# Differential keys and queries rounded on all 128 rows and placed by transfers inside SBUF

## The chip, the cores and the metric

The kernel runs on one core of one Trainium2 chip. The metric is the device time of one execution in microseconds, lower is better. Three executions of the kernel before took 2180.04, 2183.42 and 2184.76 us; their median is 2183.42 us.

## The reference

A hybrid diffusion backbone of two layers over 256 latent tokens with 256 context tokens ahead of them, width 1024. Each layer is a half-step SwiGLU feed-forward, a token mixer of two parallel branches (retention with 4 heads, differential attention with 8 heads) and another half-step feed-forward. The change lies in the keys and queries of the differential attention:

```python
def diff_attend(q, k, v, lam):
    s = jnp.einsum('bhiqd,bhikd->bhiqk', q, k).astype(jnp.float32) * (DIFF_DH ** -0.5)
    p = jax.nn.softmax(s, axis=-1)
    a = p[:, :, 0] - lam * p[:, :, 1]
    return jnp.einsum('bhqk,bhke->bhqe', a.astype(v.dtype), v)

q_d = rope_2d(to_diff_heads(dq), row, col)
k_d = rope_2d(to_diff_heads(dk), row, col)
k_dc = to_diff_heads(dkc)
k_all = jnp.concatenate([k_dc, k_d], axis=3)
```

A head has two conditions of 64 channels (the two softmax maps). Latent queries and keys are rotated in pairs of channels (a 2-D rotary embedding), context keys are not. Latent tokens read context and latent keys, context tokens context keys alone. The second layer needs no context output, so there only latent tokens have queries.

## The kernel before

**Arithmetic.** TensorE multiplies in a rounded 32-bit type. A float32 operand x is split into a rounded part H and the rest Lo = x - H, and a product is three matmuls into one PSUM bank (`mm3`, L340 to L342: H times H, H times Lo, Lo times H). Weights are loaded in 512 KB tiles by SP's queue (`load`, L147) and split by a ScalarE cast (L154) and a VectorE subtraction (L155); four raw tiles and five split tiles are in flight.

**The mixer.** `projT` (L646 ff.) makes channels x tokens blocks with the weight as the stationary operand; 48 matmuls fill one pair of PSUM banks (`main4`), which `ev` then empties, and the pair goes back to the next user. `tok` and `wide` make tokens x channels blocks with the activations as the stationary operand, 24 matmuls for a bank. The differential attention works in four blocks u = 0..3 of two heads. `diff_blocks(u)` projects and evicts K for all 512 tokens and then Q; `diff_attn` (L766 ff.) then makes for each 128 queries of a head a *score* (L781, L782: both conditions, hi and lo of the keys; L783 row maximum on VectorE; L786 two exponentials on ScalarE; L790, L792, L794 the combination of the two maps on VectorE), a *turn* (L803 transposes, L805 copy on ScalarE) and a *weigh* (L815 matmuls with V; after the last one of a block L823 square, L825 sum, L827, L829 power on GpSimd, L834 scaling). Scores, turns and weighs use the other PSUM pairs (`side4`).

**The eviction that the change touches.** In `ev_diff` (L685 to L700) the 128 rows of a block are condition 0 of a head in rows 0 to 63 and condition 1 in rows 64 to 127. For a score, the query tile of condition m holds the rounded query in 64 rows and its rest in the other 64, and the key tile holds the rounded key in both halves (and its rest in both halves of a second tile), so that two matmuls give the whole product. So each condition of K is written by a copy (L696), a subtraction (L697) and two copies into the other half (L698, L699), and each condition of Q by an activation (L692) and a subtraction into the other half (L693). Latent rows pass through `rotate` (L668, L671, L673) first, which multiplies rows with their swapped partners in pieces of 32 rows (four L671 for one block).

**What sets the order.** Work is written with deferred pieces (`defer`, `tick`, `flush`), and then a scheduler places each engine's instructions in one fixed sequence when the program is built. An engine runs its sequence in order; a matmul that waits holds all that stand behind it on TensorE. In a mixer of layer 0 the sequence of the Python code is: K(0), Q(0), deferred attention 0, `rv_block(0)` (a wide block of 96 matmuls), `rkq_blocks(0)` (the retention's key and query projections), and so on for u = 1; then K(2), Q(2), attention 2, a wide block; K(3), Q(3), attention 3, two wide blocks.

The lines that decide when the pair of a K block comes free:

```python
            for c in pairs:
                ev(c, bk[:, :, c * 256:(c + 1) * 256])
            main4.put(b0)
            tick(w)
```

Of the kernel before, what the change touches and what calls it, by code (L numbers as in the profile page):

```python
# [11 lines left out]
F32 = mybir.dt.float32  # L12
F32R = mybir.dt.float32r
BF16 = mybir.dt.bfloat16
AF = mybir.ActivationFunctionType
ALU = mybir.AluOpType
# [18 lines left out]
def build(ctx, tc, a):  # L35
# [536 lines left out]
    def mixer(l, st, AB, fetch, nxt):  # L572
# [69 lines left out]
        def projT(b, pairs, ev, w):  # L642
            ws = [split(r) for r in load(a["winT"][l, b])]
            n = 256 * len(pairs)
            if len(pairs) == 2:
                b0 = main4.two()  # L646
                bk = b0
            else:
                b0 = main4.one()
                bk = b0.rearrange("p (j n) -> p j n", j=2)  # L650
            for j in range(2):
                js = slice(j * P, (j + 1) * P)
                for k in range(KD):
                    wt = ws[k // 4].rearrange("p s (k n) -> p s k n", k=4)
                    mm3(bk[:, j], wt[:, 0, k % 4, js], wt[:, 1, k % 4, js], h[k // 2][:, k % 2, 0, 0:n],
                        h[k // 2][:, k % 2, 1, 0:n], k == 0, k == KD - 1)
                    if k == 7 and j == 0:
                        flush()
                    if j * KD + k in ((3, 7, 11) if len(pairs) == 2 else (7,)):
                        tick(w)  # L660
            for c in pairs:
                ev(c, bk[:, :, c * 256:(c + 1) * 256])
            main4.put(b0)
            tick(w)

        def rotate(b, tab, half):
            q, w = tmp2([P, 2, 256]), tmp2([P, 2, 256])
            dve.tensor_tensor(out=q, in0=b, in1=tab[:, 0].unsqueeze(1).broadcast_to([P, 2, 256]), op=ALU.mult)  # L668
            for p0 in range(0, P, half):
                p1 = p0 ^ half  # L670
                dve.tensor_tensor(out=w[p0:p0 + half], in0=b[p1:p1 + half],  # L671
                                  in1=tab[p0:p0 + half, 1].unsqueeze(1).broadcast_to([half, 2, 256]), op=ALU.mult)
            dve.tensor_tensor(out=q, in0=q, in1=w, op=ALU.add)  # L673
            return q
# [7 lines left out]
                                         op0=ALU.mult, op1=ALU.subtract)  # L682
            return ev

        def ev_diff(H, Lo):  # L685
            def ev(c, b):
                q = rotate(b, dtab, 32) if c == LAT else b
                sl = slice(c * 256, (c + 1) * 256)
                for m in range(2):
                    own, oth = slice(64 * m, 64 * m + 64), slice(64 - 64 * m, 128 - 64 * m)  # L690
                    if Lo is None:
                        act(H[m][own, :, sl], q[own], AF.Copy, scale=0.125)  # L692
                        dve.scalar_tensor_tensor(out=H[m][oth, :, sl], in0=q[own], scalar=0.125,  # L693
                                                 in1=H[m][own, :, sl], op0=ALU.mult, op1=ALU.subtract)
                    else:
                        nc.scalar.copy(H[m][own, :, sl], q[own])  # L696
                        dve.tensor_tensor(out=Lo[m][own, :, sl], in0=q[own], in1=H[m][own, :, sl], op=ALU.subtract)  # L697
                        nc.scalar.copy(H[m][oth, :, sl], q[own])  # L698
                        nc.scalar.copy(Lo[m][oth, :, sl], Lo[m][own, :, sl])  # L699
            return ev  # L700

        def ev_V(dst):
# [289 lines left out]
        def diff_blocks(u, before=None):  # L992
            KH = [slot([P, 2, 512], F32R) for _ in range(2)]
            KL = [slot([P, 2, 512], F32R) for _ in range(2)]
            projT(8 + u, BOTH, ev_diff(KH, KL), 0.3)
            if before:
                before()
            Q = [slot([P, 2, 512], F32R) for _ in range(2)]
            projT(4 + u, QP, ev_diff(Q, None), 0.3)
            return KH, KL, Q  # L1000

        def diff_defer(u, kq, dv, within):
# [223 lines left out]
def rope_tables():  # L1226
    def ang(pos, half):
        inv = (np.float32(10000.0) ** (-np.arange(half, dtype=np.float32) / np.float32(half))).astype(np.float32)
        return (pos.astype(np.float32)[:, None] * inv[None, :]).astype(np.float32)

    t = np.arange(T)
    r = ang(t, 64)
    c, s = np.cos(r), np.sin(r)
    rt = np.stack([np.concatenate([c, c], 1), np.concatenate([-s, s], 1)], 0)
    d = np.concatenate([ang(t // 64, 16), ang(t % 64, 16)], 1)
    c, s = np.cos(d), np.sin(d)
    dt = np.stack([np.concatenate([c, c, c, c], 1), np.concatenate([-s, s, -s, s], 1)], 0)

    def lay(z):
        return np.ascontiguousarray(z.transpose(2, 0, 1), dtype=np.float32)  # L1240
    return lay(rt), lay(dt)
# [6 lines left out]
def layout(i):  # L1248
    f = {k: np.asarray(v) for k, v in i.items()}
    a = {}  # L1250
    a["xin"] = np.concatenate([f["x"][0], f["ctx"][0]], 0).reshape(4, P, D)
    a["ccc"] = np.stack([f["c"][0], f["c_ctx"]], 1).reshape(KD, P, 2).transpose(1, 0, 2)
    a["sel"] = (np.arange(P)[:, None] % 32 == np.arange(2)[None, :]).astype(np.float32)
    a["wada0"] = f["w_ada"][0, :, 0:2 * D].reshape(KD, P, 2, 4, 256).transpose(3, 1, 0, 2, 4).reshape(4, P, 4096)
    a["cc"] = np.stack([f["c"][0], f["c_ctx"]], 0)
    a["wada"] = f["w_ada"].transpose(0, 2, 1).reshape(L, 36, 2, P, D).transpose(0, 1, 3, 2, 4).reshape(L, 36, P, 2 * D)
    a["bada"] = f["b_ada"].reshape(L, 9, 8, P).transpose(3, 0, 1, 2)
    a["nwc"] = f["norm_w"].reshape(L, 6, 8, P).transpose(3, 0, 1, 2)
    a["fin"] = (f["ffn_w_in"].reshape(L, 2, KD, P, 2, NF, P).transpose(0, 1, 5, 3, 2, 4, 6)
                .reshape(L, 2, NF, P, 2048))  # L1260
    a["fout"] = f["ffn_w_out"].reshape(L, 2, NF // 2, 2, P, D).transpose(0, 1, 2, 4, 3, 5).reshape(L, 2, NF // 2, P, 2048)
    cols = np.arange(8192)
    cols[3072:5120] = cols[3072:5120].reshape(32, 2, 2, 16).transpose(0, 2, 1, 3).reshape(-1)
    wi = f["w_in"][:, :, cols].reshape(L, KD, P, 32, 256)
    a["winT"] = wi[:, :, :, TB].transpose(0, 3, 2, 1, 4).reshape(L, 12, P, 2048)
    a["winW"] = wi[:, :, :, WB].reshape(L, KD, P, 10, 512).transpose(0, 3, 2, 1, 4).reshape(L, 10, P, 4096)
    a["wout"] = f["w_out"].reshape(L, 4, 2, P, D).transpose(0, 1, 3, 2, 4).reshape(L, 4, P, 2048)
    a["gnw"] = f["ret_gn_w"]
    a["subw"] = f["diff_subln_w"]
    a["lamv"] = f["diff_lambda"]  # L1270
    a["decay"] = f["ret_decay_logit"].reshape(L, 8)
    a["rtab"], a["dtab"] = rope_tables()
    a["strip"] = strip_table()
    return {k: np.ascontiguousarray(v) for k, v in a.items()}
# [16 lines left out]
```

## Time and profile before

| | before |
|---|---|
| median of 3 runs | 2183.42 us (2180.04 to 2184.76) |
| the profiled execution, own time | 2185.12 us |
| its span | 2183.3 us |
| granted TensorE clock, mean | 0.994 |
| TensorE busy (matmul) | 2140.8 us, 98% |
| VectorE busy | 1364.9 us, 63% |
| ScalarE busy | 859.4 us, 39% |
| GpSimd busy | 108.8 us, 5% |
| DMA | 306.98 MB, 141 GB/s, 41.1% of 16 engines on SP's queue |

Busy time is the sum of an engine's instructions; a matmul row shows a longer time (0.39 us for 512 columns) than the distance to the next one, since matmuls are pipelined. A timeline row has the start, the duration, engine, line, operation, tiles, and in brackets the idle time ahead of it on its engine with what ended it. In a windows row each engine's busy time stands with its number of instructions, then the granted TensorE clock (1.00 is 2.4 GHz, 0.50 is 1.2 GHz), the busy share of the DMA engines and GB/s.

### The profile page before, as it was taken

What the parts mean: (1) busy time and instruction counts of PE and PEld (TensorE: products, weight loads), DVE (VectorE), ACT (ScalarE), POOL (GpSimd) and SP (SyncE); (2) the same over time, 40 slices, a digit from 0 to 9 for tenths busy, and PEclk for the clock granted to TensorE, in tenths of its full rate; (3) what the DMA queues carried; (4) which work ended last, traced back from release to release, by engine and by line L of the source; (5) the groups of instructions that cost most, each with busy time, mean ns of one, the idle gap of its engine ahead of it and who ended that gap; (6) DMA issues with size and microseconds to landing.
All of it is one profiled execution on the core that took longest, in us unless ns stands there. A gap on an engine that the chain in (4) does not pass through costs nothing. (4 is left out here: it accounts for less than half of the span.)

```text
span 2183.3 us, 27485 instructions
## 1 busy us (share of the span) xinstructions
PE 2140.8 (98%) x10736; PEld 1792.6 (82%) x10736; DVE 1364.9 (63%) x2119; ACT 859.4 (39%) x1331; POOL 108.8 (5%) x194
## 2 busy tenths in 40 slices
PE   7999999999999999999999999999999999999998
PEld 5888888878788878888888888888888888878997
DVE  3799372677665874596233279825347776787554
ACT  3322232553534553432233252223235554565453
POOL 1000000101010000100000010000010000000000
PEclk9999999999999999999999999999999999999999
DMA  8866243222123234465234246733323323356554
GB/s 331 280 214 227 98 145 98 81 68 78 61 87 100 71 103 137 140 201 170 97 112 149 97 161 225 270 97 131 101 67 110 116 86 111 106 164 232 184 185 133
DMA packets 85058, 306.98 MB, mean 141 GB/s; under 512 B 9968, under 2 KB 10048, under 8 KB 84928
## 3 DMA queue, kind: packets, MB, share of 16 engines
q1 hardware_dynamic: 81936, 296.78, 41.1%
q0 software_dynamic: 2848, 8.43, 1.5%
q8 instruction: 84, 1.38, 0.3%
q14 instruction: 46, 0.38, 0.0%
q10 hardware_dynamic: 144, 0.01, 0.0%
HBM read 304.10 MB, written 1.09 MB: 140 GB/s over the span
## 5 line engine op out<-in xcount | busy, mean ns | idle before, releaser
L155 DVE TENSOR_TENSOR w<-raw,w 128x1024 fp32r<-128x1024 f32 x399 | 486.2, 1222 | 456.0 <-ACT w L154 452.9
L154 ACT CAST w<-raw 128x1024 fp32r<-128x1024 f32 x399 | 419.1, 1055 | 660.7 <-PE ps L342 598.2
L340 PE MATMUL ps<-h,w 128*128 128x512 f32 (+1 forms) x1820 | 652.7, 359 | 5.1 <-ACT w L154 3.0
L341 PE MATMUL ps<-h,w 128*128 128x512 f32 (+1 forms) x1820 | 652.2, 359 | 0.4 <-DVE h L293 0.3
L342 PE MATMUL ps<-h,w 128*128 128x512 f32 (+1 forms) x1820 | 651.4, 358 | 0.6 <-DVE w L155 0.6
L340 PEld LDWEIGHTS ps<-h,w 128*128 128x128 f32 x1820 | 345.2, 190 | 58.4 <-DVE h L292 4.6
L342 PEld LDWEIGHTS ps<-h,w 128*128 128x128 f32 x1820 | 345.7, 190 | 50.1 <-DVE w L155 1.3
L341 PEld LDWEIGHTS ps<-h,w 128*128 128x128 f32 x1820 | 345.7, 190 | 49.9 <-DVE h L293 1.4
L174 DVE CUSTOM_DVE_ANT_0 jd<-r,r 128x1024 bf16<-128x1024 f32 x224 | 273.4, 1220 | 5.8 <-DMA r<-wada_dram 1.6
L340 PE MATMUL ps<-w,h 128*128 128x512 f32 (+1 forms) x552 | 219.0, 398 | 16.3 <-ACT r L698 11.7
L341 PE MATMUL ps<-w,h 128*128 128x512 f32 (+1 forms) x552 | 216.8, 393 | 1.0 <-DVE w L155 1.0
L342 PE MATMUL ps<-w,h 128*128 128x512 f32 (+1 forms) x552 | 216.8, 393 | 0.0
L340 PE MATMUL ps<-w,gs 128*128 128x512 f32 x504 | 196.2, 389 | 0.0
L341 PE MATMUL ps<-w,gs 128*128 128x512 f32 x504 | 196.1, 389 | 0.0
L342 PE MATMUL ps<-w,gs 128*128 128x512 f32 x504 | 196.1, 389 | 0.0
L403 ACT ACTIVATE t<-ps 128x512 f32<-128x512 f32 (+1 forms) x85 | 46.7, 550 | 248.4 <-PE ps L342 248.4
L340 PEld LDWEIGHTS ps<-w,h 128*128 128x128 f32 x552 | 104.4, 189 | 39.8 <-ACT r L698 15.1
L341 PEld LDWEIGHTS ps<-w,h 128*128 128x128 f32 x552 | 104.4, 189 | 21.1 <-DVE w L155 2.3
L342 PEld LDWEIGHTS ps<-w,h 128*128 128x128 f32 x552 | 104.3, 189 | 20.9 <-DVE h L293 0.4
L404 DVE TENSOR_TENSOR r<-ps,t 128x512 f32<-128x512 f32 (+1 forms) x85 | 53.5, 629 | 104.1 <-PE ps L342 76.8
L340 PEld LDWEIGHTS ps<-w,gs 128*128 128x128 f32 x504 | 94.6, 188 | 20.0
L341 PEld LDWEIGHTS ps<-w,gs 128*128 128x128 f32 x504 | 94.6, 188 | 19.6
(199 smaller groups left out, 2184.4 us busy)
## 6 DMA issues: line engine op xcount, KB each, us to landing
raw<-fin_dram SPq DMA_DIRECT2D x176, 512.0 KB, 4.4
r<-wada_dram SPq DMA_DIRECT2D x144, 512.0 KB, 5.4
raw<-fout_dram SPq DMA_DIRECT2D x88, 512.0 KB, 3.6
raw<-winW_dram SPq DMA_DIRECT2D x80, 512.0 KB, 3.6
raw<-winT_dram SPq DMA_DIRECT2D x48, 512.0 KB, 3.6
raw<-wout_dram SPq DMA_DIRECT2D x16, 512.0 KB, 5.2
r<-scr POOLq DMA_DIRECT2D x10, 512.0 KB, 5.5
r<-cc_dram SPq DMA_DIRECT2D x7, 512.0 KB, 5.4
```

Of the source, the lines that this page charges most:

```text
L154: keep(nc.scalar.copy(w[:, 0, :], src))
L155: keep(dve.tensor_tensor(out=w[:, 1, :], in0=src, in1=w[:, 0, :], op=ALU.subtract))
L174: dve.tensor_tensor_reduce(out=junk, in0=r[j], in1=cs[c], scale=1.0, scalar=0.0, op0=ALU.mult, op1=ALU.add, accum_out=out[:, c, 2 * u + j: ...
L340: mm(o, lhsT=wH, rhs=xH, start=start, stop=False)
L341: mm(o, lhsT=wH, rhs=xL, start=False, stop=False)
L342: mm(o, lhsT=wL, rhs=xH, start=False, stop=stop)
L403: act(sg[:, :N], ab[0][:, :N], AF.Silu)
L404: dve.tensor_tensor(out=g[f // 2][:, f % 2, :N], in0=ab[1][:, :N], in1=sg[:, :N], op=ALU.mult)
```

## The change

The channels of the differential Q and K weight columns are permuted on the host, so that a block's rows are four groups of 32: condition 0, condition 1, condition 0, condition 1 (`rows_of`), and the partner of a row in the rotation is 64 rows away. `rotate` then needs two L671 instead of four. `ev_full` rounds all 128 rows at once: one activation and one subtraction for each of context and latent. The 32-row groups are then put where the scores want them by transfers from SBUF to SBUF on SP's queue (`move`): six moves of two transfers for K (128 KB each), four moves of two for Q; the third K move overwrites rows that the first two read. Q's rounded rows and rests go through two more slots of the big ring (qH, qL). `projT` evicts the context columns first, the latent ones after. No matmul is added or removed.

```diff
-            for c in pairs:
+            for c in reversed(pairs):
                 ev(c, bk[:, :, c * 256:(c + 1) * 256])
...
-        def ev_diff(H, Lo):
+        def rows_of(m):
+            return [slice(32 * m + 64 * x, 32 * m + 64 * x + 32) for x in range(2)]
+
+        def move(dst, md, src, ms, n):
+            for rd, rs in zip(rows_of(md), rows_of(ms)):
+                nc.sync.dma_start(dst[rd, :, 0:n].bitcast(F32), src[rs, :, 0:n].bitcast(F32))
+
+        def ev_full(H, Lo, scale):
             def ev(c, b):
-                q = rotate(b, dtab, 32) if c == LAT else b
+                q = rotate(b, dtab, 64) if c == LAT else b
                 sl = slice(c * 256, (c + 1) * 256)
-                for m in range(2):
...
+                act(H[:, :, sl], q, AF.Copy, scale=scale)
+                dve.scalar_tensor_tensor(out=Lo[:, :, sl], in0=q, scalar=scale, in1=H[:, :, sl],
+                                         op0=ALU.mult, op1=ALU.subtract)
             return ev
...
-            projT(8 + u, BOTH, ev_diff(KH, KL), 0.3)
+            projT(8 + u, BOTH, ev_full(KH[0], KL[0], 1.0), 0.3)
+            for K2 in (KH, KL):
+                move(K2[1], 1, K2[0], 1, 512)
+                move(K2[1], 0, K2[0], 1, 512)
+                move(K2[0], 1, K2[0], 0, 512)
...
-            projT(4 + u, QP, ev_diff(Q, None), 0.3)
+            qH, qL = slot([P, 2, 512], F32R), slot([P, 2, 512], F32R)
+            projT(4 + u, QP, ev_full(qH, qL, 0.125), 0.3)
+            for m in range(2):
+                move(Q[m], m, qH, m, 256 * NQ)
+                move(Q[m], 1 - m, qL, m, 256 * NQ)
+            slots.put(qH, qL)
             return KH, KL, Q
```

In the changed kernel the attention's lines are one lower than before (L782 is the maximum, L793 the combination, L802 the transposes, L804 the copy, L814 the weigh, L824 the sum), the moves are L690, the evictions' activation and subtraction L696 and L697.

TensorE, layer 0, u = 0: the first scores. Before, they stand 35 matmuls behind the Q projection (names: `ps` is PSUM, `w` a split weight, `h` the activations, the numbered `r` are slots of the big ring):

```order
L340 MATMUL ps<-w,h 128x512
L341 MATMUL ps<-w,h 128x512
L781 MATMUL ps<-r_3118,r_3204 128x512 [waits DVE_49]
L782 MATMUL ps<-r_3120,r_3204 128x512
L781 MATMUL ps<-r_3119,r_3205 128x512 [waits DVE_49]
L782 MATMUL ps<-r_3121,r_3205 128x512
```

Now they wait on the transfers, and stand behind 96 matmuls of the wide block and 4 of the next projection:

```order
L342 MATMUL ps<-w,h 128x512
L340 MATMUL ps<-h,w 128x512 [waits DVE_49]
L341 MATMUL ps<-h,w 128x512
L342 MATMUL ps<-h,w 128x512
L340 MATMUL ps<-h,w 128x512
L780 MATMUL ps<-r_3118,r_3202 128x512 [waits DMAHW4_49,DMAHW7_49,DMAHW1_49,DMAHW0_49]
L781 MATMUL ps<-r_3120,r_3202 128x512 [waits DMAHW6_49,DMAHW5_49]
```

So the block's eight scores moved from the wide block into the retention's key and query projections behind it.

TensorE, the same block's end: the last weigh. Before, it has projection matmuls on both sides, 17 ahead of it and 60 behind it:

```order
L340 MATMUL ps<-h,w 128x512
L341 MATMUL ps<-h,w 128x512
L342 MATMUL ps<-h,w 128x512
L815 MATMUL ps<-r_2895,t_3597 128x128 [waits Activation_49]
L815 MATMUL ps<-r_2895,t_3597 128x128
L340 MATMUL ps<-h,w 128x512
L341 MATMUL ps<-h,w 128x512
```

Now the last two turns and weighs follow each other, and the wide block of the retention's gates comes directly behind, waiting for VectorE:

```order
L342 MATMUL ps<-h,w 128x512
L802 MATMUL ps<-ident,t_3535 128x128 [waits DVE_49,Activation_49]
L802 MATMUL ps<-ident,t_3535 128x128
L814 MATMUL ps<-r_2895,t_3593 128x128 [waits Activation_49]
L814 MATMUL ps<-r_2895,t_3593 128x128
L802 MATMUL ps<-ident,t_3567 128x128 [waits DVE_49]
L802 MATMUL ps<-ident,t_3567 128x128
L814 MATMUL ps<-r_2895,t_3599 128x128 [waits Activation_49]
L814 MATMUL ps<-r_2895,t_3599 128x128
L340 MATMUL ps<-w,h 128x512 [waits DVE_49]
```

VectorE at that place now. The L340 above waits for the second L671 here, the last reading of the pair of the retention's key block; ahead of it stands the sum L824, which waits for ScalarE's square of the last weigh:

```order
L793 SCALAR_TENSOR_TENSOR t_3567<-t_3567,r_3572 128x256 [waits DVE_49]
L681 SCALAR_TENSOR_TENSOR r_3689<-ps,r_3688 128x2x256 [waits Activation_49]
L155 TENSOR_TENSOR w<-raw,w 128x1024 [waits DMAHW3_49,Activation_49]
L668 TENSOR_TENSOR t_3680<-ps,rtab 128x512
L824 TENSOR_REDUCE oss<-t_3653 128x4 [waits Activation_49]
L671 TENSOR_TENSOR t_3681<-ps,rtab 64x512
L826 SCALAR_TENSOR_TENSOR ms<-oss,es 128x4 [waits DVE_49]
L671 TENSOR_TENSOR t_3681<-ps,rtab 64x512
L833 SCALAR_TENSOR_TENSOR r_3661<-ps,rr,sub 128x128 [waits PE_49,Pool_49]
```

Before, the sum and the scaling of the block are done on VectorE ahead of that eviction:

```order
L155 TENSOR_TENSOR w<-raw,w 128x1024 [waits DMAHW4_49,Activation_49]
L825 TENSOR_REDUCE oss<-t_3651 128x4 [waits Activation_49]
L827 SCALAR_TENSOR_TENSOR ms<-oss,es 128x4 [waits DVE_49]
L834 SCALAR_TENSOR_TENSOR r_3659<-ps,rr,sub 128x128 [waits PE_49,Pool_49]
L834 SCALAR_TENSOR_TENSOR r_3659<-ps,rr,sub 128x128 x3
L668 TENSOR_TENSOR t_3676<-ps,rtab 128x512 [waits PE_49]
L671 TENSOR_TENSOR t_3677<-ps,rtab 64x512 x2
```

So the sum of the block moved from ahead of the eviction of the retention's keys into the middle of it. TensorE, layer 1, u = 2, the end of the attention now (K(3) and Q(3) are projected ahead of it, a wide block follows):

```order
L342 MATMUL ps<-h,w 128x256
L802 MATMUL ps<-ident,t_14177 128x128 [waits DVE_49]
L802 MATMUL ps<-ident,t_14177 128x128 x3
L814 MATMUL ps<-r_13741,t_14229 128x128 [waits Activation_49]
L814 MATMUL ps<-r_13741,t_14229 128x128
L814 MATMUL ps<-r_13742,t_14229 128x128 x2
L802 MATMUL ps<-ident,t_14201 128x128 [waits DVE_49]
L802 MATMUL ps<-ident,t_14201 128x128 x3
L814 MATMUL ps<-r_13741,t_14239 128x128 [waits Activation_49]
L814 MATMUL ps<-r_13741,t_14239 128x128
L814 MATMUL ps<-r_13742,t_14239 128x128 x2
L340 MATMUL ps<-w,h 128x512 [waits DVE_49]
```

Before, the last weigh there stands 59 matmuls ahead of that wide block:

```order
L815 MATMUL ps<-r_13725,t_14219 128x128 [waits Activation_49]
L815 MATMUL ps<-r_13725,t_14219 128x128
L815 MATMUL ps<-r_13726,t_14219 128x128 x2
L340 MATMUL ps<-h,w 128x512
L341 MATMUL ps<-h,w 128x512
```

So this attention's last turns and weighs moved behind both projections.

## Rows read from the trace of the kernel before

**Rows 1.** The page, part 1: busy time, share of the span, instructions.

```profile
PE 2140.8 (98%) x10736; PEld 1792.6 (82%) x10736; DVE 1364.9 (63%) x2119; ACT 859.4 (39%) x1331; POOL 108.8 (5%) x194
```

**Rows 2.** Waits of TensorE: line, releaser, us in total, times, longest.

```profile
PE ps L340 <- ACT r L698: 11.7, 8, 1.7
PE ps L340 <- DVE t L671: 3.2, 1, 3.2
```

**Rows 3.** Timeline of TensorE in layer 0, u = 0: the Q projection's end.

```profile
446.48 0.39 PE L340 MATMUL ps<-h,w 128*128 128x512 f32 x1
...
446.93 0.39 PE L342 MATMUL ps<-h,w 128*128 128x512 f32 x1
...
448.97 0.50 PE L340 MATMUL ps<-w,h 128*128 128x512 f32 x1 [1.65 <-ACT r L698]
```

**Rows 4.** Timeline of TensorE in layer 1: two long waits and what follows.

```profile
1916.15 0.60 PE L340 MATMUL ps<-w,h 128*128 128x512 f32 x1 [3.16 <-DVE t L671]
1917.58 0.80 PE L340 MATMUL ps<-w,h 128*128 128x512 f32 x1 [0.82 <-ACT r L698]
1918.17 0.63 PE L341 MATMUL ps<-w,h 128*128 128x512 f32 x1
...
1922.44 0.63 PE L342 MATMUL ps<-w,h 128*128 128x512 f32 x1
...
1966.17 0.66 PE L982 MATMUL ps<-ident,t 128*128 128x128 f32 x4 [2.05 <-DVE t L975]
```

**Rows 5.** Windows around a short and the two long waits.

```profile
445.00:455.00 10.00, 8.35 (x37) 6.58 (x36) 7.11 (x9) 6.37 (x11) 0.00 (x0) 1.00 0.18 55
...
1918.00:1921.00 3.00, 3.00 (x8) 2.33 (x8) 2.85 (x4) 1.88 (x4) 0.00 (x0) 0.50 0.36 98
...
1965.00:1970.00 5.00, 3.83 (x14) 3.14 (x15) 4.92 (x6) 3.63 (x6) 0.00 (x0) 0.75 0.97 326
```

**Rows 6.** Windows over four attentions: layer 0 u = 0, 2, 3, layer 1 u = 3.

```profile
457.00:497.00 40.00, 39.87 (x212) 31.90 (x212) 26.08 (x52) 20.99 (x51) 1.95 (x1) 1.00 0.17 55
...
717.00:752.00 35.00, 34.83 (x191) 27.92 (x191) 27.90 (x59) 19.74 (x49) 1.04 (x1) 1.00 0.13 41
778.00:815.00 37.00, 36.32 (x200) 28.99 (x200) 29.56 (x58) 21.18 (x52) 3.06 (x3) 1.00 0.28 87
...
1922.00:1943.00 21.00, 20.85 (x110) 16.80 (x109) 16.68 (x26) 13.49 (x28) 0.00 (x0) 0.97 0.43 137
```

**Rows 7.** Groups of instructions: count, busy us, mean ns, idle before.

```profile
L155 DVE TENSOR_TENSOR w<-raw,w 128x1024 fp32r<-128x1024 f32 x399 | 486.2, 1222 | 456.0 <-ACT w L154 452.9
...
L671 DVE TENSOR_TENSOR t<-ps,dtab 32x512 f32<-32x512 f32 x64 | 44.0, 687 | 0.9
...
L699 ACT CAST r<-r 64x512 fp32r<-64x512 f32 x32 | 19.8, 618 | 0.5
...
L697 DVE TENSOR_TENSOR r<-ps,r 64x512 fp32r<-64x512 f32 x16 | 11.0, 689 | 13.4 <-ACT r L696 13.1
L671 DVE TENSOR_TENSOR t<-ps,rtab 64x512 f32<-64x512 f32 x16 | 11.0, 688 | 0.2
...
L825 DVE TENSOR_REDUCE oss<-t 128x4 f32<-128x512 f32 x12 | 8.1, 679 | 2.1 <-ACT t L823 2.1
...
L823 ACT ACTIVATE t<-ps 128x512 f32<-128x512 f32 x12 | 7.2, 596 | 1.6 <-PE ps L815 1.6
...
L964 DVE SCALAR_TENSOR_TENSOR t<-t,ps 128x512 f32<-128x512 f32 x6 | 4.1, 682 | 0.6 <-ACT t L963 0.5
```

**Rows 8.** DMA issues: KB each, median us to landing; one issue's time.

```profile
raw<-winT_dram SPq DMA_DIRECT2D x48, 512.0 KB, 3.6
...
out_dram<-X SPq DMA_DIRECT2D x4, 256.0 KB, 2.1
rtab<-rtab_dram SPq DMA_DIRECT2D x1, 256.0 KB, 11.2
...
1979.84 0.33 SPq L163 DMA_DIRECT2D r<-cc_dram  x1
```

More of the change, by code (lines that the diff above doesn't have):

```diff
@@ L683, in ev_ret @@
             return ev
-        def ev_diff(H, Lo):
+        def rows_of(m):
[4 more added lines that the diff above has]
+        def ev_full(H, Lo, scale):
             def ev(c, b):
-                q = rotate(b, dtab, 32) if c == LAT else b
+                q = rotate(b, dtab, 64) if c == LAT else b
                 sl = slice(c * 256, (c + 1) * 256)
-                for m in range(2):
[L690 to L699, printed above, removed]
+                act(H[:, :, sl], q, AF.Copy, scale=scale)
+                dve.scalar_tensor_tensor(out=Lo[:, :, sl], in0=q, scalar=scale, in1=H[:, :, sl],
+                                         op0=ALU.mult, op1=ALU.subtract)
             return ev
@@ L1236, in rope_tables @@
     c, s = np.cos(d), np.sin(d)
-    dt = np.stack([np.concatenate([c, c, c, c], 1), np.concatenate([-s, s, -s, s], 1)], 0)
+    dt = np.stack([np.concatenate([c, c, c, c], 1), np.concatenate([-s, -s, s, s], 1)], 0)
     def lay(z):
@@ L1262, in layout @@
     cols = np.arange(8192)
-    cols[3072:5120] = cols[3072:5120].reshape(32, 2, 2, 16).transpose(0, 2, 1, 3).reshape(-1)
+    cols[3072:5120] = cols[3072:5120].reshape(16, 2, 2, 2, 16).transpose(0, 3, 1, 2, 4).reshape(-1)
     wi = f["w_in"][:, :, cols].reshape(L, KD, P, 32, 256)
```

## The prediction, made before the changed kernel ran

> **What bounds the kernel now.** I read the busy times first. TensorE works 98% of the span, VectorE 63%, ScalarE 39% [rows 1]: only what makes TensorE wait, or slows its clock, moves the time; work saved on the two others is worth nothing by itself. So the second view is what TensorE waits for [rows 2]. Eight of its waits, 11.7 us together, end on L698, the copy that empties the keys' PSUM pair last; one of 3.2 us ends on the rotation of a query block (L671). Third, the timeline of the first of them [rows 3]: two matmuls are 0.45 us apart over two steps, so one takes 0.227 us of TensorE's time, and a Q projection of 48 takes 10.9 us. After its last matmul at 446.93 the next starts at 448.97, 2.04 us later instead of 0.227: a wait listed as 1.65 costs 1.81, 0.16 more than its row says. The Q projection is what covers K's eviction, and the cover is just too short. Fourth, the two long waits of layer 1 [rows 4] and the clock after them [rows 5]: after 3.16 and 0.82 us of idling the matmuls from 1918.17 to 1922.44 are 0.427 apart at a granted clock of 0.50, which is 1.2 GHz; after 2.05 us at 1966.17 the window grants 0.75 in the mean. Around the wait of 1.65 us the clock stays at 1.00.
>
> **What the change takes away.** (1) The eviction. 120 ScalarE copies and activations of 0.62 us [rows 7] become 28, and some 60 VectorE operations of 0.69 us, half of the 64 quarter-row L671 and about half of the subtractions (56 become 28), go: 60 x 0.69 = 41 us of VectorE. Neither engine bounds, so this counts at nothing but for the waits. The context goes first now, so the pair is read for the last time by the rotation of the latent half: one subtraction, one L668 and two L671, 4 x 0.69, and a weight split L155 of 1.22 that may stand between, 4.0 us. That is under the 10.9 us of the Q projection, and under the 5.5 us that it takes with half as many columns in layer 1 (an estimate, half of 10.9). So the eight waits go: 11.7 us and 8 x 0.16 = 1.3. (2) The 3.2 us at 1916.15 go too, since the work around it is laid out anew, and with it the slow stretch: the eleven steps from 1917.58 to 1922.44 took 4.86 us instead of 11 x 0.227 = 2.5, so 2.4. Sum of the gains: 11.7 + 1.3 + 3.2 + 2.4 = **18.6 us**.
>
> **What it adds on SP's queue.** 20 transfers for each of eight blocks, at 0.33 us for an issue [rows 8]: 6.6 us of SP's time a block, in front of later weight loads, which have to wait until Q's eviction is through. The nine tiles in flight cover it: one feeds 24 matmuls, 5.45 us. No row shows a transfer inside SBUF. The nearest, by size, is 2.1 us for 256 KB from SBUF; the far end is 11.2 us for the table at the start. I take 2.1 to 3.6; a score needs K's third move behind the first two, and Q's. The 100 matmuls (22.7 us) that now lie between Q's projection and the first score hold even two landings of 11.2 us. So the transfers themselves cost nothing, with 0 and some 5 us for a block as the ends. The Trainium skill, "DMA: Bandwidth & Descriptors", section "Rules for kernel authors", speaks against this change: it advises to gather many small transfers into one large one, and "SBUF — State Buffer", section "Door 1: The DMA port swizzle", has 32 neighbouring rows reach half of the ports only. By these a move would land later than rows of its size say; the sum above would still be zero as long as the 22.7 us hold, and no run here shows such a transfer yet.
>
> **What it adds on TensorE: the order.** The scheduler knows that the scores now wait for transfers and has set them further back: behind 100 matmuls instead of 35 in block 0. The attention's chain of score, maximum, exponential, combination, turn, copy, weigh is long and crosses three engines; TensorE gets through it only where other matmuls stand between. I counted in the built order the projection matmuls between a block's first score and last weigh. Layer 0: 97, 97, 79, 89 before; 92, 92, 68, 64 now. Layer 1: 48, 43, 41, 58 before; 36 and 33 of half width, 51, 36 of half width only, and 27 now. Those that are gone, at 0.227: 1.1 + 1.1 + 2.5 + 5.7 in layer 0; in layer 1 nothing for the first two, 41 x 0.227 - 36 x 0.114 = 5.2, and 31 x 0.227 = 7.0. Sum **22.6 us** of cover, all of which becomes idling if the chains ran without slack. They have some: VectorE is busy 65%, 80% and 80% of the time in three such stretches of layer 0 and 79% in layer 1's last [rows 6]. If it could be filled fully, only the last would still lose, 16.7 - (21 - 7.0) = 2.7 us, and I put the lower end at 7 with two others that lose their cover in one piece. On the other side the cover left has moved forward: in block 0 40 of 92 now stand ahead of the second pair of scores (24 of 97 before), so 52 instead of 73 lie later, 4.8 us less and not 1.1; counted so for all eight the sum is 35. I take 24, near the count, since the maxima and splits leave VectorE little room where the cover goes in one piece (layer 0, u = 2: 30 rows without one other matmul).
>
> **The ends of three attentions** are dearer. Behind the last weigh of u = 0 and u = 1 in layer 0 the next matmul waits for the retention keys' eviction, and that now has the block's sum in its middle: L823's square 0.60, L825 0.68, two L671 1.38 [rows 7] make 2.7 us in which TensorE has nothing. Where a split (1.22) and two evictions of 0.69 are still ahead on VectorE it is up to 5.3. I take 3.5 for each. In layer 1, u = 2, the next matmul waits for L964 behind that sum: 0.60 + 0.68 + 0.68 = 2.0, and the second wait 16 matmuls later, for the rotation behind the power and the scaling, adds some 0.6. Sum 3.5 + 3.5 + 2.6 = **9.6 us** (7.4 to 14).
>
> **The clock.** These idle stretches are 2 us and more, as the two in [rows 4]. Each of those brought a stretch at 1.2 GHz that cost about 2 (2.4 above). For four of them 8 us, between 2 and 16.
>
> **Sum.** 9.6 + 24 + 8 - 18.6 = +23.0 us. The profiled execution took 2185.12 us, 1.7 above the median of 2183.42; on the median the forecast is 2183.4 + 23.0 = **2206 us**. The low ends give 7.4 + 7 + 2 - 18.6 = -2.2, so 2181; the high ends 14 + 35 + 16 - 18.6 = +46.4, so 2230.
>
> **Rivals.** *Faster: the chains hold.* If VectorE's slack (20 to 35%) takes up the shifted cover and the ends wait only for what is done anyway, the L698 waits are gone and nothing replaces them: 2183.4 - 13.0 to 18.6 = 2165 to 2170, say 2169. For it: 41 us less on VectorE, and TensorE hardly idles in these stretches now (39.87 of 40.00). Against it: the three ends are fixed in the order, 7.4 us at least. It decides from the point where tails, chains and clock together lose less than the 18.6 us. Chance 0.22. *A draw*, the same loss as gain within 0.2% (4.4 us, what a measurement of this kernel can tell from no change): 2183; 0.08. *Transfers late.* A score waits on DMA and SP's queue holds weight loads behind moves: 5 us a block and more, 2206 + 8 x 5 = 2246. For it: the queue is one, and moves wait in it for evictions; against it: 22.7 us of cover. 0.05. *The clock rules.* If all eight attentions idle often enough to run at 1.2 GHz for longer, the projections between, some 60 matmuls a block on average, take 0.2 us more for a third of them: 4 us x 8 = 32, so 2206 - 8 + 32 = 2230. Against it: waits of 1.65 us leave the clock at 1.00. The Trainium skill, "TensorE: Matmul & The Clock Gate", section "HAM oscillation — how this bites in real kernels", describes a kernel that pays for a slow clock again at each wait; the two long waits here agree, the eight short ones don't show it. 0.07. *The change does nothing*, the order leaving the L698 waits in place: excluded by the counts, within the draw.
>
> **Numbers.** Forecast (2206, its own range 2190 to 2222) 0.58; faster 0.22, draw 0.08, clock 0.07, transfers 0.05. Slower by over 0.2%: 0.58 + 0.07 + 0.05 = 0.70. Range 2168 to 2232: it takes in the sum's ends, the draw, the clock's case and the upper half of the faster one (2165 to 2170 and what lies above); outside remain 0.11 of that case, the late transfers 0.05 and the rest above 2232.
>
> **What would show it.** No wait on an eviction's copy behind the Q projections; in the list of TensorE's waits new ones on L793, L785, L804 (the chain) and on L671 of the retention's key table, the latter twice near 3 us; half-clock stretches behind them; transfers of 128 KB landing under 4 us and few waits on DMA. It is wrong if TensorE's idle time in the eight attentions stays under 15 us, or if the scores wait on transfers.

## The result, and the profile after

| | before | changed |
|---|---|---|
| median | 2184.09 us (2180.04 to 2185.12, 4 runs) | 2215.43 us (2213.03 to 2216.56, 4 runs) |
| span of the profiled execution | 2183.3 us | 2213.8 us |
| granted TensorE clock, mean | 0.994 | 0.986 |

The ratio is 1.0151 with a 95% interval of 1.0139 to 1.0163: the change makes the kernel 31 us slower. Where the spans part: the first matmul of the feed-forward's second product behind layer 0's mixer starts at 1145.01 before and at 1161.68 after, so layer 0's mixer has 16.7 of the 30.5 us; the rest, 13.8, lies in layer 1's. (Below, that start is the mark for the end of layer 0's mixer.)

The page of the changed kernel, part 1:

```profile
PE 2152.8 (97%) x10736; PEld 1808.8 (82%) x10736; DVE 1317.8 (60%) x2059; ACT 801.8 (36%) x1239; POOL 110.4 (5%) x194
```

Against [rows 1] VectorE lost 47 us of work and ScalarE 58, as the change meant; what that is worth shows only without the transfers (e2). TensorE runs the same 10736 matmuls, yet is busy 12.0 us longer; its idle time, span less busy, went from 42.5 to 61.0. These two make the 30.5 us. (Matmul rows overlap, and TensorE's busy time counts each moment once: it is the time in which at least one matmul runs, not the sum of its rows.)

What TensorE waits for in the changed kernel (us in total, times, longest):

```profile
PE ps L340 <- DVE t L671: 6.0, 2, 3.0
PE ps L341 <- DVE w L155: 4.3, 3, 2.9
PE ps L342 <- DVE w L155: 3.6, 2, 2.9
PE ps L981 <- ACT t L804: 3.6, 1, 3.6
PE ps L814 <- ACT t L804: 3.3, 6, 0.7
PE ps L780 <- ACT t L785: 3.0, 1, 3.0
...
PE ps L340 <- DVE t L963: 2.9, 2, 2.0
...
PE ps L981 <- ACT t L785: 2.3, 1, 2.3
```

The eight waits on L698 [rows 2] are gone. In their place stand the ends of the attentions (L671 twice 3.0, L963 2.0) and the attention's own chain: maximum, exponential, combination, turn, copy. No score waits for a transfer. Four attentions as in [rows 6], layer 0 u = 0, 2, 3 and layer 1 u = 3, each from its first score to its last weigh, show the idle time as the window less TensorE's busy time, 1.8, 4.5, 3.5 and 6.5 us:

```profile
469.80:508.20 38.40, 36.60 (x197) 29.86 (x195) 25.73 (x51) 20.28 (x49) 1.04 (x1) 0.98 0.27 86
739.20:777.30 38.10, 33.63 (x173) 27.47 (x171) 24.58 (x51) 18.57 (x48) 1.04 (x1) 0.91 0.18 60
811.00:846.80 35.80, 32.33 (x186) 25.29 (x185) 26.83 (x54) 20.77 (x53) 2.52 (x3) 1.00 0.24 72
1958.30:1984.80 26.50, 19.98 (x101) 16.58 (x99) 19.48 (x28) 17.42 (x32) 0.00 (x0) 0.87 0.46 154
```

The end of block 0, the timeline of all engines:

```profile
506.96 1.22 PE L814 MATMUL ps<-r,t 128*128 128x128 f32 x4 [0.52 <-ACT t L804]
507.58 0.68 DVE L668 TENSOR_TENSOR t<-ps,rtab 128x512 f32<-128x512 f32 x1
508.27 0.60 ACT L822 ACTIVATE t<-ps 128x512 f32<-128x512 f32 x1 [1.37 <-PE ps L814]
508.90 0.69 DVE L824 TENSOR_REDUCE oss<-t 128x4 f32<-128x512 f32 x1 [0.64 <-ACT t L822]
509.62 0.69 DVE L671 TENSOR_TENSOR t<-ps,rtab 64x512 f32<-64x512 f32 x1
510.23 0.15 DVE L826 SCALAR_TENSOR_TENSOR ms<-oss,es 128x4 f32<-128x4 f32 x1
510.41 0.68 DVE L671 TENSOR_TENSOR t<-ps,rtab 64x512 f32<-64x512 f32 x1
...
511.15 0.79 PE L340 MATMUL ps<-w,h 128*128 128x512 f32 x1 [2.97 <-DVE t L671]
511.74 0.63 PE L341 MATMUL ps<-w,h 128*128 128x512 f32 x1
```

This is the row-by-row form of the built order: last weigh, square, then VectorE waits 0.64 us for that square although the L671 behind it could run, and TensorE stands still for 2.97 us. The matmuls behind it take 0.63 instead of 0.39, the half clock. Windows show it (TensorE, its weights, VectorE, ScalarE, GpSimd, granted clock, DMA). The clock had fallen before the long wait: it was 0.50 from 506.8 on, behind waits of 0.80, 0.46 and 0.52 us. The same holds in layer 1's block 2, where it was 0.50 from 1926.8 on, behind waits of 1.24 and 0.68 us, and stayed so past the wait of 2.0 us that ended at 1933.38:

```profile
504.50:506.70 2.20, 1.34 (x8) 0.89 (x8) 1.81 (x7) 1.48 (x3) 0.00 (x0) 1.00 0.66 192
506.80:508.20 1.40, 1.22 (x4) 0.93 (x4) 1.40 (x2) 0.10 (x1) 0.00 (x0) 0.50 0.17 64
...
511.00:515.00 4.00, 3.85 (x9) 3.07 (x10) 3.58 (x9) 1.34 (x2) 1.03 (x2) 0.50 0.16 49
515.00:520.00 5.00, 5.00 (x20) 4.05 (x20) 4.27 (x9) 2.11 (x4) 0.00 (x0) 0.80 0.00 2
...
1926.80:1931.00 4.20, 3.52 (x17) 3.12 (x16) 0.83 (x2) 0.58 (x1) 0.00 (x0) 0.50 0.53 187
...
1934.00:1938.00 4.00, 4.00 (x13) 3.15 (x12) 3.54 (x10) 0.00 (x0) 0.49 (x1) 0.63 0.00 0
```

Inside an attention the chain shows like this, layer 0, block 2 and layer 1, block 2:

```profile
745.31 0.39 PE L781 MATMUL ps<-r,r 128*128 128x512 f32 x1
...
748.71 0.50 PE L780 MATMUL ps<-r,r 128*128 128x512 f32 x1 [3.01 <-ACT t L785]
...
1909.79 2.35 DVE L782 TENSOR_REDUCE mx<-ps 128x2 f32<-128x1024 f32 x2 [1.50 <-PE ps L781]
...
1912.06 1.21 DVE L155 TENSOR_TENSOR w<-raw,w 128x1024 fp32r<-128x1024 f32 x1
...
1913.33 0.58 PE L342 MATMUL ps<-h,w 128*128 128x256 f32 x1 [2.89 <-DVE w L155]
```

At 748.71 a third score waits for the exponentials (L785) of the two ahead of it, and no projection stands between. At 1913.33 it is a projection that waits: its weight split stands behind two row maxima on VectorE.

And the transfers, SP's queue around block 0, and the DMA issues (KB each, median us to landing):

```profile
442.33 17.10 SPq L690 DMA_DIRECT2D r<-r  x20
459.47 0.58 SPq L147 DMA_DIRECT2D raw<-winT_dram  x1
```

```profile
r<-r SPq DMA_DIRECT2D x128, 128.0 KB, 2.3
```

The twenty issues of block 0 take SP's queue 17.1 us, from the first key to the last query, waits for the evictions included; one issue takes 0.58 us (the median of all 160). The last one starts at 458.8 and lands 2.3 us later, about 461.1; the first score starts at 469.8. So the scores of this block stand some 8.7 us, 38 matmuls, further back than the data asks.

### The profile page after: what moved, and what is told of

The parts are those of the page before. It is cut to its first block, busy times and chain, and to the rows that moved or that the text cites. A ratio compares the mean times of both kernels' runs of the same rounds, so it can differ in the third digit from the quotient of the medians.

```text
span 2213.8 us, 27591 instructions
## 1 busy us (share of the span) xinstructions
PE 2152.8 (97%) x10736; PEld 1808.8 (82%) x10736; DVE 1317.8 (60%) x2059; ACT 801.8 (36%) x1239; POOL 110.4 (5%) x194
## 5 line engine op out<-in xcount | busy, mean ns | idle before, releaser
L340 PE MATMUL ps<-h,w 128*128 128x512 f32 (+1 forms) x1820 | 653.8, 360 | 5.9 <-ACT w L154 3.0
L340 PEld LDWEIGHTS ps<-h,w 128*128 128x128 f32 x1820 | 345.5, 190 | 58.7 <-DVE h L292 4.7
L340 PE MATMUL ps<-w,h 128*128 128x512 f32 (+1 forms) x552 | 218.9, 398 | 9.4 <-DVE t L671 6.0
L340 PE MATMUL ps<-w,gs 128*128 128x512 f32 x504 | 196.3, 389 | 0.0
L340 PEld LDWEIGHTS ps<-w,h 128*128 128x128 f32 x552 | 105.8, 192 | 31.9 <-DVE t L671 6.8
L340 PEld LDWEIGHTS ps<-w,gs 128*128 128x128 f32 x504 | 94.6, 188 | 20.0
```

What stands on the lines that cost most here:

```text
L340: mm(o, lhsT=wH, rhs=xH, start=start, stop=False)
```

## The experiments

Two theories. **Place**: the loss comes from where the scheduler puts the scores behind the transfers; the gain comes from a pair that is free in time. Rivals: the **transfers** themselves (number, landing, SP's queue held), or the **eviction** (full rows, rotation, its order) costs the time. Times are medians, ratios to the kernel before with their 95% intervals; beside the experiments the kernel before took 2182.1 to 2183.1 us.

### e1: only the order of eviction

```diff
-            for c in pairs:
+            for c in reversed(pairs):
                 ev(c, bk[:, :, c * 256:(c + 1) * 256])
```

> The kernel before with one line changed: a K block evicts its context columns first, its latent ones after; no full-row rounding, no transfers. Theory (the loss comes from the place of the scores behind the transfers, the gain from an earlier free PSUM pair): the waits of TensorE on L698 go (11.7 us and 1.3 for the restarts), the wait of 3.2 us at the end of layer 1 may stay; the scores stay some 36 to 48 matmuls behind the Q projection, projection matmuls between first score and last weigh fall by 41 in all eight blocks (9 us of cover at most): 2166 to 2180, say 2172. Rival (the copies, not their order, hold the pair): the L698 waits stay, 2180 to 2186.

2173.05 us, ratio 0.9953 (0.9939 to 0.9968). TensorE's waits:

```profile
PE ps L340 <- DVE t L671: 5.3, 8, 1.0
```

As expected (2166 to 2180): the L698 waits are gone with one line; eight waits on the rotation remain, at most 1.0 us each. A part of the change alone is faster than before.

### e2: the change without its transfers

```diff
-            for K2 in (KH, KL):
-                move(K2[1], 1, K2[0], 1, 512)
-                move(K2[1], 0, K2[0], 1, 512)
-                move(K2[0], 1, K2[0], 0, 512)
...
-            projT(4 + u, QP, ev_full(qH, qL, 0.125), 0.3)
-            for m in range(2):
-                move(Q[m], m, qH, m, 256 * NQ)
-                move(Q[m], 1 - m, qL, m, 256 * NQ)
-            slots.put(qH, qL)
+            projT(4 + u, QP, ev_full(Q[0], Q[1], 0.125), 0.3)
```

(and the scores read `KH[0]`, `KL[0]` for both conditions)

> The changed kernel without the 160 transfers: the scores read the rounded rows and rests directly where they were evicted, so the products of the differential scores are left wrong and the placing is left out. Theory (the transfers, by the place that the scores get behind them, cost the time): scores stand 13 to 17 matmuls further up than in the changed kernel by some 60 to 70, ends and weaves are covered again: 2163 to 2172. Rival (the full-row eviction, the new rotation or the order of the eviction cost it): above 2200.

2162.16 us, ratio 0.9903 (0.9889 to 0.9918), 0.8 us below what I expected. The page, part 1:

```profile
PE 2132.5 (99%) x10736; PEld 1790.1 (83%) x10736; DVE 1320.7 (61%) x2059; ACT 801.3 (37%) x1239; POOL 109.7 (5%) x194
```

So full-row eviction, rotation, permutation and the reversed order together are worth 21 us, and the transfers take 53 us from there to 2215. Against this run the changed kernel's TensorE is busy 20.3 us longer and idle 34.2 longer (61.0 against 26.8). This clears the eviction as the cause, but not yet the transfers themselves.

### e3: the same transfers on ScalarE's queue

```diff
-                nc.sync.dma_start(dst[rd, :, 0:n].bitcast(F32), src[rs, :, 0:n].bitcast(F32))
+                nc.scalar.dma_start(dst[rd, :, 0:n].bitcast(F32), src[rs, :, 0:n].bitcast(F32))
```

> The changed kernel with the same transfers issued by ScalarE's queue instead of SP's. In the built order the first scores then stand some 20 matmuls further up, and between first score and last weigh there are 97, 97, 91, 79, 48, 48, 36 and 20 of half width, 47 projection matmuls, near those of the kernel before. Theory (place of the scores): most of the loss goes, 2172 to 2195, with issue time on ScalarE and some end waits left. Rival (the transfers' own time, their landing or their traffic): stays at 2210 to 2220.

2182.53 us, ratio 1.0001 (0.9992 to 1.0011): the same bytes in the same pieces, 33 us less. Its waits begin with

```profile
PE ps L780 <- DMA r<-r: 12.4, 2, 6.8
```

Two scores of layer 1 now wait for transfers (5.55 us at 1877.89 and 6.82 at 1928.15). Layer 0's mixer ends at 1137.8, 24 us ahead of the changed kernel and 7 ahead of the kernel before; layer 1 gives those 7 back. There the place is too early, in the changed kernel it is too late.

### e4: the change with latent columns first

```diff
-            for c in reversed(pairs):
+            for c in pairs:
                 ev(c, bk[:, :, c * 256:(c + 1) * 256])
```

> The changed kernel with the old order of eviction, latent columns first. Theory: the full-row eviction alone frees the pair in time, in some 6 us of the Q projection's 10.9 in layer 0, and the order of the scores is nearly that of the changed kernel: 2211 to 2222, no wait on the eviction in layer 0. Rival (the reversed order is what moved the scores and ends): below 2205.

2205.03 us, ratio 1.0099 (1.0084 to 1.0114): below what I expected by 6, just at the rival's edge. The ends stay: two waits of 3.4 us for the retention keys' L681 instead of two of 3.0 for L671.

```profile
PE ps L340 <- DVE r L681: 7.0, 3, 3.4
```

The page, part 1:

```profile
PE 2143.9 (97%) x10736; PEld 1800.1 (82%) x10736; DVE 1319.2 (60%) x2059; ACT 804.3 (37%) x1239; POOL 108.4 (5%) x194
```

So the reversal, which alone gains 10 us on the old eviction (e1), loses 10 beside the full-row one, and most of the loss is there without it. Of the 11.9 us between the spans of the two profiled executions (2201.9 here), 8.9 are busy time of the same matmuls at a mean granted clock of 0.992 against 0.986, and only 3.0 are idling (58.0 against 61.0). What in the order makes the clock fall more often with it stays open.

### e5: rotate first, then context, then latent, on the kernel before

```diff
+            rot = pre(bk[:, :, LAT * 256:(LAT + 1) * 256]) if pre else None
-            for c in pairs:
-                ev(c, bk[:, :, c * 256:(c + 1) * 256])
+            for c in reversed(pairs):
+                ev(c, rot if pre and c == LAT else bk[:, :, c * 256:(c + 1) * 256])
```

> The kernel before with the latent rotation of K put ahead of both evictions, then context, then latent; copies and subtractions as before, no transfers. Theory: the last reading of the pair is now a copy or subtraction of the context columns instead of the L671 behind them, so the eight waits on L671 that context-first alone left (5.3 us with 1.3 for restarts) shrink to under 2 us, while the scores stay where they were: 2163 to 2171, say 2168. Rival (VectorE's subtractions wait for ScalarE's copies all the same): 2171 to 2177, as context-first alone.

(K and Q both pass their rotation to `projT` as `pre`, and the eviction no longer calls it.) 2170.46 us, ratio 0.9942 (0.993 to 0.9955), within the range, but its interval overlaps that of e1: the 2.6 us between them are not clear of noise. And the waits did not shrink to under 2 us. Layer 0 has no such wait left; in layer 1, where the Q projection is half as long, four remain:

```profile
PE ps L340 <- ACT r L699: 4.8, 4, 3.2
```

### e6: the change with two queues

```diff
-                nc.sync.dma_start(dst[rd, :, 0:n].bitcast(F32), src[rs, :, 0:n].bitcast(F32))
+                eng.dma_start(dst[rd, :, 0:n].bitcast(F32), src[rs, :, 0:n].bitcast(F32))
```

(`eng` is ScalarE's queue for the rounded rows, KH and qH, and SP's for the rests, KL and qL)

> The changed kernel with the rounded rows moved by ScalarE's queue and the rests by SP's. In the built order the first scores then stand at the 1988th matmul in block 0 (2027 in the changed kernel, 1962 before), with 82, 82, 92, 93, 46, 46, 36 and 16 of half width, 48 projection matmuls to the last weigh. Theory (the place of the scores): 2168 to 2186, with waits on transfers at the end of layer 1 at most, each under 4 us. Rival (a larger number of queues changes nothing, the transfers' own time counts): 2205 to 2220.

2163.56 us, ratio 0.9913 (0.9899 to 0.9927): **faster than both kernels, with every transfer in place**, 4 us below what I expected, and 1.4 us from the run without any. The page, part 1, the waits on transfers and their landing:

```profile
PE 2131.2 (99%) x10736; PEld 1791.0 (83%) x10736; DVE 1316.4 (61%) x2059; ACT 798.9 (37%) x1239; POOL 110.6 (5%) x194
```

```profile
PE ps L780 <- DMA r<-r: 1.0, 1, 1.0
```

```profile
r<-r ACTq DMA_DIRECT2D x64, 128.0 KB, 4.3
r<-r SPq DMA_DIRECT2D x64, 128.0 KB, 4.0
```

A transfer lands later than in the changed kernel (4.0 to 4.3 us against 2.3), and the kernel is 52 us faster: landing is not what costs. With two queues the first scores of block 0 stand 39 matmuls further up. The cover between first score and last weigh is not larger everywhere: in blocks 0 and 1 of layer 0 it is 82 matmuls, against 92 in the changed kernel, yet the mixer of layer 0 ends 28 us earlier (1133.96). There the place of the cover differs, above all at the end: between the last two turns and weighs stand 5 and 3 projections (none in the changed kernel), and the matmul behind the last weigh does not wait.

### e7 and e8: both kernels with TensorE in the written order

```diff
-        st = mixer(l, st, AB1, F1, AB2)
+        with tc.manual_schedule(engines={nc.tensor.engine}):
+            st = mixer(l, st, AB1, F1, AB2)
```

> The kernel before with TensorE's instructions of both mixers kept in the order in which the code is written, so that the scores stand at fixed places, 12 projection matmuls apart, the first ones 12 behind the Q projection. Reference for the next run. The L698 waits stay (13 us), and a score 12 matmuls (2.7 us) behind the Q projection waits for Q's eviction, some 3 us a block: 2190 to 2230.

2346.43 us, ratio 1.0752 (1.0736 to 1.0769), far above what I expected: fixed places leave no room for the evictions and for the attention's chain. TensorE idles 156.5 us instead of 42.5, and is busy 52 us longer at a mean granted clock of 0.968. The largest waits are

```profile
PE ps L340 <- ACT r L698: 34.1, 8, 6.9
PE ps L340 <- DVE t L901: 28.1, 20, 5.2
PE ps L781 <- DVE r L693: 18.1, 4, 4.5
```

> The changed kernel with TensorE in the written order, the same places as in the run above, so that the transfers cannot move the scores. Theory: transfers take from the end of the Q projection to landing some 4 to 6 us of eviction, 2.6 of issue, 2.3 of landing, 9 to 11 us, of which 12 matmuls cover 2.7: 6 to 8 us of waits on transfers a block in layer 0, 4 to 6 in layer 1, 45 us together, less the 13 of L698: 20 to 45 us above the run in the written order without transfers. Rival (transfers are quick enough, the scheduler placed the scores back for nothing): within 10 us of it or below.

2386.58 us, ratio 1.0933 (1.0916 to 1.095): 40 us above e7, inside the 20 to 45 expected, in part by luck: I took 45 us of waits on transfers and 13 that go, and both are larger. Here the transfers cannot move the scores, and they show:

```profile
PE ps L780 <- DMA r<-r: 85.5, 16, 10.8
```

The L698 waits (34.1) and 18.1 of waits for the queries' subtraction go; 85.5 - 34.1 - 18.1 = 33 of the 40, and TensorE idles 33.7 us more than in e7. So placed at once behind the projection, the transfers on one queue do hold the scores, twice in each block. The scheduler had a reason to move them, only it moved them further than needed (by the 8.7 us above, in block 0).

### e9 and e10: only the queries' transfers, only the keys'

The edit of e9 (the scores read `KH[0]`, `KL[0]`, as in e2):

```diff
-            for K2 in (KH, KL):
-                move(K2[1], 1, K2[0], 1, 512)
-                move(K2[1], 0, K2[0], 1, 512)
-                move(K2[0], 1, K2[0], 0, 512)
```

And of e10, where the eviction writes into `Q` directly, as in e2:

```diff
-            for m in range(2):
-                move(Q[m], m, qH, m, 256 * NQ)
-                move(Q[m], 1 - m, qL, m, 256 * NQ)
```

> The changed kernel with the queries' transfers alone (64 of 160); the keys' six moves a block are left out, and both conditions read the keys' tile as it was evicted, so the products of the scores are left wrong. In the built order the first scores of block 0 stand at the 1990th matmul (2027 in the changed kernel, 1962 before) with 92, 92, 100, 100, 46, 46, 44, 62 projection matmuls up to the last weigh. Theory (one queue serves keys', then queries' transfers, then weight loads in order, and the scores are placed by its length): most of the loss goes with the keys' transfers, 2162 to 2175. Rival (the transfers behind the Q projection cost the time, as the scores wait for the queries'): 2195 or more.

2159.10 us, ratio 0.9895 (0.988 to 0.991), 3 us below what I expected and as fast as e2 within the intervals. A query's rest then meets the other condition's keys, so this is no version of the kernel, but its time tells: the 64 transfers that come last before the scores cost nothing.

> The changed kernel with the keys' transfers alone (96 of 160); the queries' rounded rows and rests are read where they were evicted, so the products of the scores are left wrong. First scores at the 1956th matmul. Theory: the keys' transfers are through behind the 10.9 us of the Q projection, the scores stand as early as before: 2160 to 2175, with a few short waits on transfers. Rival (the third move of the keys, which waits for the first two, holds SP's queue and with it scores or weights): 2185 or more.

2179.03 us, ratio 0.9983 (0.9973 to 0.9992), 4 us above what I expected. No wait on a transfer. Layer 0 gains fully (its mixer ends at 1132.3); in layer 1 the attention of block 2 starts 70 matmuls further up than in the changed kernel, but ends behind both projections again, with waits of 2.0 us on L963 and 2.9 on a split. So the queries' transfers alone cost nothing, the keys' alone 17 of the 53 us, and the rest comes only when both stand in one queue.

### e11: twice the transfers

```diff
-                nc.sync.dma_start(dst[rd, :, 0:n].bitcast(F32), src[rs, :, 0:n].bitcast(F32))
+                for j in range(2):
+                    nc.sync.dma_start(dst[rd, j, 0:n].bitcast(F32), src[rs, j, 0:n].bitcast(F32))
```

> The changed kernel with every transfer cut into two of half the size (320 instead of 160). The built order hardly differs: first scores at the 2023rd matmul (2027), and 96, 96, 72, 71, 34, 35, 0 and 30 projection matmuls of full width to the last weigh (92, 92, 68, 64, 36, 51, 0, 27). Theory (the place decides, not the transfers themselves): 2207 to 2225, few or no waits on transfers. Rival (the number of transfers, issue and fixed times, costs): 2235 or more, with waits on transfers or late weights.

2218.70 us, ratio 1.0168 (1.0153 to 1.0183), which overlaps the changed kernel's interval. 160 transfers more cost some 3 us, which is not clear of noise, though some scores do begin to wait:

```profile
PE ps L781 <- DMA r<-r: 9.0, 4, 3.7
```

### e12: keys on SP's queue, queries on ScalarE's

```diff
-                move(Q[m], m, qH, m, 256 * NQ)
-                move(Q[m], 1 - m, qL, m, 256 * NQ)
+                move(Q[m], m, qH, m, 256 * NQ, nc.scalar)
+                move(Q[m], 1 - m, qL, m, 256 * NQ, nc.scalar)
```

> The changed kernel with the keys' transfers on SP's queue and the queries' on ScalarE's. First scores at the 1990th matmul, 101, 101, 100, 119, 76, 76, 37 and 48 of half width, 67 projection matmuls to the last weigh. Theory: as with the rounded rows and the rests on two queues, 2162 to 2175. Rival (only the split of rows and rests, by which the third move's wait is halved, helps): 2185 or more.

2180.93 us, ratio 0.9993 (0.9984 to 1.0003): a miss, 6 us above the theory and 4 below the rival, and as slow as the keys' transfers alone (e10). Layer 0 gains fully again (its mixer ends at 1132.2), layer 1 shows what e10 showed:

```profile
PE ps L341 <- DVE w L155: 4.6, 3, 2.9
...
PE ps L340 <- DVE t L963: 2.0, 1, 2.0
```

Two queues help only if they bring the scores forward in both layers; split by rounded rows and rests they do (e6), split by keys and queries the attention of layer 1's block 2 still ends right ahead of the wide block. In the trace the second product of a score there (L781, with the keys' rests, the last keys that SP's queue moves) stands 17 and 33 projection matmuls behind its first (L780) in the first scores; in e6 it stands directly behind.

## Why the prediction was right, point by point

**Direction and size.** 2206 was forecast with 2168 to 2232; 2215.4 came. Forecast +23.0 us, measured +30.5 in the span. The signs named for it came too: waits on L793, L785 and L804, the two on L671 near 3 us, the half clock, and transfers that land in under 4 us with no score waiting for one.

**What it takes away.** As said: no L698 wait is left, and the pair of block 0 is read for the last time well inside the Q projection. The 18.6 us of gains agree with e2, which shows 21 with the transfers out.

**SP's queue: nothing.** Right for the changed kernel: no score waits for a transfer, and 128 KB land in 2.3 us, inside the 2.1 to 3.6 that I took. An issue takes 0.58 us and not 0.33, which cost nothing here. The Trainium skill's advice in "DMA: Bandwidth & Descriptors", section "Rules for kernel authors", to gather small transfers was no guide to the loss: twice as many cost some 3 us, not clear of noise (e11), the same ones on two queues gain 52 (e6).

**The order.** Right, and the runs show it: e3 and e6 keep the work and the transfers, change the place of the scores, and get 33 and 52 us back. The ends were taken at 3.5, 3.5 and 2.6 and are 2.97, 2.98 and 2.0 us; the second wait expected in layer 1 did not come; the first eight of the 16 matmuls in front of it ran at half clock, which gave it time. The lost cover was taken at 24. From first score to last weigh TensorE idles 1.8, 1.8, 4.5 and 3.5 us in layer 0 and 0, 0, 5.5 and 6.5 in layer 1, 23.6 in all, against 1.4 before; the count had 1.1, 1.1, 2.5, 5.7 and 0, 0, 5.2, 7.0, so its sum is right and its sizes are nearly so. With the ends that is twice the 15 us under which the prediction would have been wrong.

**The clock: the mis-sized term.** I took 8 us for four idle stretches, less 2.4 for the old one, so 5.6. TensorE's busy time rose by 12.0 for the same matmuls. The half clock sets in at more places than the ends: the two mixers have eight stretches at 0.50, which set in near 506.8, 633.0, 749.1, 1913.0, 1926.7, 1964.2, 1977.9 and 1995.0, against two before (1916.3 and 1967.5). And not all of them follow an idle stretch of 2 us, as I had it: three (506.8, 1926.7, 1995.0) set in behind two or three shorter waits, none over 1.41 us, for which I had no clock cost. Behind 748.71 (3.01 us idle) the eight matmuls of a weigh, 1.05 us at full clock, take 1.91. The last of the eight, before and behind its start:

```profile
1991.00:1994.90 3.90, 1.26 (x7) 0.83 (x7) 3.90 (x7) 2.58 (x3) 0.63 (x1) 1.00 0.22 89
1995.10:1998.00 2.90, 2.90 (x10) 2.45 (x9) 2.54 (x4) 0.59 (x1) 0.00 (x0) 0.50 0.95 316
```

The 6.4 us missing here are most of the 7.5 us between forecast and result.

**Rivals.** *Chains hold* is what happens when the scores are moved back less or not at all (e2, e6, e9: 2159 to 2164, below the 2169 that I gave it). *Transfers late* is real where the scores stand early: 12.4 us in e3, 85.5 in e8. *The clock rules* had the direction of the miss: the clock falls in five of the eight attentions, and the busy time shows 12 us for it, not 32.

**What stays open.** The runs show that the queue decides the place and that the place decides the time. They do not show how long the scheduler takes a transfer to be, nor which of its rules sets the place. No run puts the scores at the changed kernel's places without any transfer; that the place costs and not the transfers rests on the list of waits, in which no score waits for one, and on e3, e6 and e9.

## What to carry to other kernels

A transfer that is hidden can still cost, if a scheduler fixes the order when the program is built: compare the built order of both versions on the critical engine before looking at any duration, and count the cover between a chain's first and last step, and look at where in it the cover lies (e6 has less of it in two blocks and loses nothing there). Where data has to be placed by transfers in front of such a chain, try several splits over two queues: by rounded rows and rests it gave 52 us here, by keys and queries 34. And when a change bundles several edits, try each alone: one line of this one (e1) was worth 10 us by itself.

## What the runs showed that I had not expected

- With two queues (e6) 128 KB land in 4.0 to 4.3 us, with one in 2.3, and the two are still far better for the kernel.
- Waits of the same length need not bring the same clock. In layer 1's block 2, e4 and the changed kernel have the same order of matmuls and the same waits within 0.01 us (2.89, then 1.24, 0.68, 0.68 and 2.00). Behind the first of them the changed kernel runs at 0.50, e4 at 1.00; e4's clock falls only at 1922.1. And in e6 TensorE waits 2.09 us up to 1932.82 and stays at 1.00. So whether a given wait costs the clock could not be told here from its length. The changed kernel, e4 and e6 in turn:

```profile
1913.10:1916.40 3.30, 3.07 (x12) 2.88 (x13) 2.27 (x7) 1.66 (x4) 0.00 (x0) 0.50 0.46 159
...
1906.20:1916.00 9.80, 8.78 (x66) 8.15 (x66) 9.59 (x14) 8.41 (x17) 0.00 (x0) 1.00 0.59 182
...
1930.00:1933.00 3.00, 0.91 (x5) 0.44 (x4) 0.92 (x3) 2.25 (x4) 0.00 (x0) 1.00 0.65 191
1933.00:1936.00 3.00, 3.00 (x18) 2.61 (x19) 3.00 (x5) 3.00 (x5) 0.00 (x0) 1.00 0.25 82
```

- Reversing the order of eviction helps one kernel by 10 us and hurts the other by 10 (e1, e4).
